# One batch of ring addresses per loop round, in place of an address instruction before each operation, in a streaming RMSNorm + swish kernel

## The chip, the cores and the metric

The kernel runs on one core of one Trainium2 chip. The metric is the device time of one execution in microseconds. Three runs of the kernel before gave 159.98, 160.04 and 160.12 us; their median, 160.04 us, is the time that the change is measured against. One further execution was recorded by the hardware profiler, and all rows of the profile come from it: it took 159.97 us, of which the span from the first to the last instruction is 158.5 us.

## What is computed

The input x has 16 x 1024 rows of 512 float32. Each row is divided by its root mean square, multiplied by gamma (512 values), and passed through swish:

```python
rms = np.sqrt(np.mean(x ** 2, axis=-1, keepdims=True) + eps)
x_norm = x / rms * gamma
return x_norm * (1.0 / (1.0 + np.exp(-x_norm)))
```

Input and output are 33.55 MB each, so 67.1 MB have to cross between the chip's memory and the core.

## The kernel before, in words

The 16,384 rows are laid over the 128 partitions, 128 rows to a partition. A row of a partition is 512 floats (2 KB). On the chip stands one buffer, `xb`, a ring with room for 96 of the 128 rows of every partition; rows 96 to 127 go into the places of rows 0 to 31 once these have been stored. All work on a row is done in place in `xb`.

The transfers are all issued by SyncE (SP), in an order written out by hand (lines 30 to 41): seven loads fill the ring (rows 0-3, 4-7, 8-15, 16-31, 32-63, 64-91, 92-95), the first two of them ahead of the program's opening barrier. SP then waits until the load of rows 64-91 has landed (line 156), issues the stores of rows 0-15 and 16-31 (line 138), waits for each of these two before it issues the loads that reuse its places (line 132), waits for the load of rows 112-123 (line 156), and then issues the five last stores: rows 32-63, 64-95, 96-111, 112-119 and 120-127. Every store also waits on the semaphore `s_swish`, which counts finished units; a unit is 4 rows of every partition. The five last stores need 16, 24, 28, 30 and 32 of the 32 units. At the end SP waits for the stores to land (line 277).

The compute is software pipelined over the 32 units. For each unit:

- `square` on ScalarE (ACT), lines 191 to 201: rows 2 and 3 are each squared and summed by an activation of 512 elements whose output goes to a scratch tile `junk` (line 193); rows 0 and 1 are squared by one activation of 1024 elements into the PSUM tile `sq` (line 199). It waits on `s_land`, which TensorE's queue raises as loads land (line 166).
- `sums` on VectorE (DVE), line 220: sums `sq` over the two rows into `ms`.
- `power` on GpSimd (POOL), lines 175 and 182: `rstd` = (ms + eps) to the power -1/2.
- `norm` on DVE, line 230: four operations, one for each row, multiply the row by its `rstd` and by gamma in place.
- `swish` on ACT, line 205: one activation of 2048 elements in place, which raises `s_swish`.

ACT and DVE each run a hardware loop of 10 rounds with `turn` = 3 units to the round (lines 244 and 256); two units are squared ahead of the loop and two are finished behind it (`lead` = 2). In a round ACT does, three times over, the square of unit m + 2 and then the swish of unit m; DVE does the sums of unit m + 1 and then the norm of unit m. At the end of a round each engine takes the round's counts off its semaphores (line 161), adds one to its counter and branches back.

Since the ring place of a unit depends on the round, the operations in the loops address `xb` through a register. `now` and `then` are row numbers held in registers; `rows(at, n)` makes a slice out of one, and the compiler puts ahead of each operation a fused register instruction that multiplies the row number out to a byte address (it shows as FUSED_REGOPS in the trace, with the line number of the operation that it serves). The units ahead of and behind the loops have fixed addresses and no such instructions.

Of the kernel before, what the change touches and what calls it, by code (L numbers as in the profile page):

```python
# [9 lines left out]
def kernel(  # L10
# [7 lines left out]
    nc = tc.nc  # L18
    P = nc.NUM_PARTITIONS
    AF = mybir.ActivationFunctionType  # L20
    ALU = mybir.AluOpType
    fp32 = mybir.dt.float32
# [3 lines left out]
    R, D = xf.shape  # L26

    groups = [16, 16, 32, 32, 16, 16]
    ring = 96
# [13 lines left out]
    cn = 4  # L43
    n_sq = 2
    turn = 3
    lead = 2
# [14 lines left out]
    per_ring = ring // (turn * cn)  # L61
# [15 lines left out]
    def sbuf(name, shape, dt=fp32):  # L77
        return nc.alloc_sbuf_tensor(name, shape, dt).ap()

    xb = sbuf("xb", [P, ring, D])  # L80
    gamma4 = sbuf("gamma4", [P, D])
    gamma_sb = sbuf("gamma_sb", [P, D])
    neg_half = sbuf("neg_half", [P, cn])
# [2 lines left out]
    rstd = sbuf("rstd", [P, turn, cn])  # L86
    sq = [nc.alloc_psum_tensor(f"sq{i}", [P, n_sq, D], fp32).ap() for i in range(turn)]
    junk = [nc.alloc_psum_tensor(f"junk{i}", [P, D], fp32).ap() for i in range(2)]
    junk += [sbuf(f"junk{i}", [P, D]) for i in range(2, turn * (cn - n_sq))]

    ld = [nc.alloc_semaphore(f"ld{t}") for t in range(len(loads))]
# [5 lines left out]
    s_land = nc.alloc_semaphore("s_land")  # L97
# [8 lines left out]
    def need(ins, sem, value):  # L106
        return ins.wait_op(sem, value, "sem-ge")
# [36 lines left out]
    for t in range(early):  # L144
# [3 lines left out]
        at = next(  # L148
            i for i, other in enumerate(entry)
            if other.engine == mybir.EngineType.SP  # L150
            and isinstance(other, mybir.InstDrain)
        )
# [7 lines left out]
    def take(queue, sem, n):  # L160
        need(queue.nop(nofuse=True), sem, n).then_inc(sem, -n)
# [24 lines left out]
        ).then_inc(s_rstd, 1)  # L186

    def rows(at, n):
        return xb[:, at : at + n, :] if isinstance(at, int) else xb[:, bass.ds(at, n), :]

    def square(k, at, sem, count, accs):
        for j in range(n_sq, cn):
            acc = nc.scalar.activation(  # L193
                out=junk[(k % turn) * (cn - n_sq) + j - n_sq], in_=rows(at + j, 1)[:, 0, :], func=AF.Square,
                scale=inv_d**0.5, accum_out=ms[:, k % turn, j : j + 1],
            )
            if j == n_sq:
                need(acc, sem, count)
        nc.scalar.activation(  # L199
            out=sq[k % turn], in_=rows(at, n_sq), func=AF.Square, scale=inv_d**0.5,  # L200
        ).then_inc(s_sq, 1)

    def swish(at, nth):
        need(
            nc.scalar.activation(out=rows(at, cn), in_=rows(at, cn), func=AF.Silu),  # L205
            s_norm, nth + 1,
        ).then_inc(s_swish, 1)
# [5 lines left out]
    nc.scalar.preload_act_table_set("silu_and_others")  # L213
    for k in range(lead):
        assert landings[k] == [k]
        square(k, k * cn, ld[k], 16, k * (cn - n_sq))

    def sums(k, nth):
        need(
            nc.vector.tensor_reduce(  # L220
                out=ms[:, k % turn, 0:n_sq], in_=sq[k % turn], op=ALU.add,
                axis=mybir.AxisListType.X,
            ),
            s_sq, nth + 1,
        ).then_inc(s_sum, 1)

    def norm(k, at, nth):
        for j in range(cn):
            row = rows(at + j, 1)[:, 0, :]
            ins = nc.vector.scalar_tensor_tensor(  # L230
                out=row, in0=row, scalar=rstd[:, k % turn, j : j + 1], in1=gamma_sb,
                op0=ALU.mult, op1=ALU.mult,
            )
            if j == 0:
                need(ins, s_rstd, nth + 1)
        ins.then_inc(s_norm, 1)
# [4 lines left out]
    ).then_inc(s_gamma, 1)  # L241
    nc.vector.wait_ge(s_gamma, 1)

    with nc.Fori(0, rounds, engines=[mybir.EngineType.Activation]) as i:  # L244
        now = nc.scalar.snap((i % per_ring) * (turn * cn))
        then = nc.scalar.snap(((i + 1) % per_ring) * (turn * cn))
        for m in range(turn):
            behind = now + (m + lead) * cn if m + lead < turn else then + (m + lead - turn) * cn
            square(m + lead, behind, s_land, m + 1, lead * (cn - n_sq) + m * (cn - n_sq))
            swish(now + m * cn, m)  # L250
        take(nc.scalar, s_land, turn)
        take(nc.scalar, s_norm, turn)
    for m in range(lead):
        swish((rounds * turn + m) * cn % ring, m)

    with nc.Fori(0, rounds, engines=[mybir.EngineType.DVE]) as i:
        now = nc.vector.snap((i % per_ring) * (turn * cn))
        for m in range(turn):
            sums(m + 1, m + 1)
            norm(m, now + m * cn, m)  # L260
        take(nc.vector, s_sq, turn)
        take(nc.vector, s_rstd, turn)
    sums(K - 1, 1)
    for m in range(lead):
        norm(rounds * turn + m, (rounds * turn + m) * cn % ring, m)
# [47 lines left out]
```

## Time and profile before

| | |
|---|---|
| median of three runs | 160.04 us (159.98 to 160.12) |
| the profiled execution | 159.97 us |
| its span, first to last instruction | 158.5 us |
| ACT busy | 129.7 us (82% of the span) |
| DVE busy | 124.5 us (79%) |
| POOL busy | 65.4 us (41%) |
| moved by DMA | 67.12 MB, mean 424 GB/s over the span |
| end of the last swish | 143.8 us into the span |

Busy times are those of the engines' own operations. Register, branch, semaphore and DMA-issuing instructions are handled by an engine's sequencer and are not counted as busy; where a view lists them, the engine's name carries a q (ACTq, DVEq, SPq). "DMA" in the views by windows is the busy share of the core's 16 DMA engines, where 1.00 is all of them all the time; a packet counts in the window in which it is booked, so that short windows read over or under the mean.

### The profile page before, as it was taken

The page shows a single profiled execution, that of the slowest core. Times are in us where ns is not written, and L with a number is a line of the kernel's source. Part 1 is how long each engine was busy: PE and PEld are TensorE (multiplying, and loading weights), DVE is VectorE, ACT ScalarE, POOL GpSimd, SP SyncE. Part 2 cuts the span into 40 slices and gives each one's busy share as a digit, 9 for nine tenths or more (in the row PEclk, how much of TensorE's full clock was granted, in tenths as well). Part 3 has the DMA queues.
Part 4 walks back from the last instruction along what each step waited for, and adds up shares of the span by engine and source line. Part 5 has one row for each costly group of instructions (what it writes and reads, how often), then busy time and mean ns, then how long its engine had stood idle before and what let it go on. Part 6 is the DMA issues. An engine that isn't in the chain of part 4 may idle for free. (4 is left out here: it accounts for less than half of the span.)

```text
span 158.5 us, 896 instructions
## 1 busy us (share of the span) xinstructions
DVE 124.5 (79%) x162; ACT 129.7 (82%) x193; POOL 65.4 (41%) x70
## 2 busy tenths in 40 slices
DVE  0187968999199999999999999999999999980000
ACT  0949959995599999999999999999999999663000
POOL 1053555555055555555555555555555555500000
DMA  7999997989999969999999999896996996999996
GB/s 256 445 492 397 397 612 314 529 380 414 463 463 463 405 279 440 513 414 397 397 455 463 407 428 529 364 529 281 513 529 265 529 513 281 405 496 414 389 414 265
DMA packets 2456, 67.12 MB, mean 424 GB/s; under 512 B 276, under 2 KB 276, under 8 KB 280
## 3 DMA queue, kind: packets, MB, share of 16 engines
q1 hardware_dynamic: 2448, 67.11, 98.6%
q10 hardware_dynamic: 8, 0.01, 0.0%
HBM read 33.56 MB, written 33.55 MB: 424 GB/s over the span
## 5 line engine op out<-in xcount | busy, mean ns | idle before, releaser
L230 DVE SCALAR_TENSOR_TENSOR xb<-xb,rstd,gamma_sb 128x512 f32 (+1 forms) x128 | 87.3, 744 | 0.0
L205 ACT ACTIVATE xb<-xb (+1 forms) x32 | 60.9, 1903 | 2.8 <-DVE xb L230 2.8
L220 DVE TENSOR_REDUCE ms<-sq 128x2 f32<-128x1024 f32 x32 | 39.2, 1224 | 17.4 <-ACT sq L199 14.2
L175 POOL TENSOR_SCALAR aeps<-ms 128x4 f32<-128x4 f32 x32 | 20.6, 643 | 69.0 <-DVE ms L220 69.0
L182 POOL TENSOR_TENSOR rstd<-aeps,neg_half 128x4 f32<-128x4 f32 x32 | 44.1, 1378 | 2.7
L193 ACT ACTIVATE junk<-xb 128x512 f32 (+1 forms) x64 | 38.6, 603 | 7.7 <-PEq L166 7.5
L199 ACT ACTIVATE sq<-xb 128x1024 f32 (+1 forms) x32 | 32.2, 1005 | 0.0
L193 ACT ACTIVATION_READ_ACCUMULATOR junk<-xb 128x1 f32 x64 | 11.9, 186 | 0.0
L213 ACT ACT_TABLE_LOAD x1 | 1.3, 1283 | 3.6 <-issue 3.6
L168 POOL MEMSET gamma<- 128x512 f32 x1 | 0.5, 524 | 1.5 <-POOLq L75 1.5
L240 DVE STREAM_SHUFFLE gamma_sb<-gamma 128x512 f32<-128x512 f32 x1 | 0.7, 719 | 0.0
L294 POOL MEMSET const-float32-0.0<- 128x1 f32 x1 | 0.1, 98 | 0.2 <-issue 0.2
L294 POOL MEMSET const-uint8-127<- 128x1 uint8 x1 | 0.1, 102 | 0.0
L294 POOL MEMSET const-bfloat16-1.0<- 128x1 bf16 x1 | 0.1, 101 | 0.0
L169 POOL MEMSET neg_half<- 128x4 f32 x1 | 0.1, 101 | 0.0
L294 POOL MEMSET const-float32-1.0<- 128x1 f32 x1 | 0.1, 98 | 0.0
L240 DVE LOAD_MASK_SELECT gamma_sb<-gamma x1 | 0.0, 14 | 0.0
## 6 DMA issues: line engine op xcount, KB each, us to landing
out_dram<-xb SPq DMA_DIRECT2D x3, 4096.0 KB, 19.5
xb<-in_x_dram SPq DMA_DIRECT2D x2, 4096.0 KB, 19.6
xb<-in_x_dram SPq DMA_DIRECT2D x1, 7168.0 KB, 54.8
xb<-in_x_dram SPq DMA_DIRECT2D x4, 1024.0 KB, 13.0
out_dram<-xb SPq DMA_DIRECT2D x2, 2048.0 KB, 15.5
xb<-in_x_dram SPq DMA_DIRECT2D x1, 3072.0 KB, 16.9
xb<-in_x_dram SPq DMA_DIRECT2D x1, 2048.0 KB, 10.2
out_dram<-xb SPq DMA_DIRECT2D x2, 23.9
```

The costliest lines, as they stand in the source:

```text
L168: nc.gpsimd.memset(gamma4, 0.0).then_inc(s_zero, 1)
L169: nc.gpsimd.memset(neg_half, -0.5).then_inc(s_half, 1)
L175: nc.gpsimd.tensor_scalar(out=aeps[:, m, :], in0=ms[:, m, :], scalar1=eps_f, scalar2=None, op0=ALU.add,),
L182: nc.gpsimd.tensor_tensor(out=rstd[:, m, :], in0=aeps[:, m, :], in1=neg_half, op=ALU.pow),
L193: acc = nc.scalar.activation(out=junk[(k % turn) * (cn - n_sq) + j - n_sq], in_=rows(at + j, 1)[:, 0, :], func=AF.Square, scale=inv_d**0.5 ...
L199: nc.scalar.activation(out=sq[k % turn], in_=rows(at, n_sq), func=AF.Square, scale=inv_d**0.5,).then_inc(s_sq, 1)
L205: nc.scalar.activation(out=rows(at, cn), in_=rows(at, cn), func=AF.Silu),
L213: nc.scalar.preload_act_table_set("silu_and_others")
L220: nc.vector.tensor_reduce(out=ms[:, k % turn, 0:n_sq], in_=sq[k % turn], op=ALU.add, axis=mybir.AxisListType.X,),
L230: ins = nc.vector.scalar_tensor_tensor(out=row, in0=row, scalar=rstd[:, k % turn, j : j + 1], in1=gamma_sb, op0=ALU.mult, op1=ALU.mult,)
L240: nc.vector.stream_shuffle(gamma_sb, gamma4, [0] * 32), s_gld, 16
L294: nc = _bacc.Bacc("TRN2", target_bir_lowering=False, num_devices=1)
```

## The change

The ring is allocated as bytes and viewed as float32, so that an operation can be given a byte address that already stands in a register. `now` and `then` become byte offsets. At the head of each round a new function, `addresses`, asks for all the addresses of the round at once, and the compiler packs up to six of the additions into one fused register instruction. The operations then use the finished registers.

```diff
+    row = D * mybir.dt.size(fp32)
+    xb8 = sbuf("xb", [P, ring * row], mybir.dt.uint8)
+    xb = xb8.bitcast(fp32).rearrange("p (r d) -> p r d", d=D)
...
     def rows(at, n):
-        return xb[:, at : at + n, :] if isinstance(at, int) else xb[:, bass.ds(at, n), :]
...
+        if isinstance(at, int):
+            return xb[:, at : at + n, :]
+        base, c = at
+        return bass.AP(
+            xb8.tensor, base + c * row, xb8[:, 0 : n * row].ap
+        ).bitcast(fp32)
+
+    def addresses(queue, base, offsets):
+        for c in offsets:
+            nc.lower_val(base + c * row + 16512, [queue])
...
+    span = turn * cn
     with nc.Fori(0, rounds, engines=[mybir.EngineType.Activation]) as i:
-        now = nc.scalar.snap((i % per_ring) * (turn * cn))
-        then = nc.scalar.snap(((i + 1) % per_ring) * (turn * cn))
+        now = nc.scalar.snap((i % per_ring) * (span * row))
+        then = nc.scalar.snap(((i + 1) % per_ring) * (span * row))
+        ahead = [
+            (now, m * cn) if m < turn else (then, m * cn - span)
+            for m in range(lead, lead + turn)
+        ]
+        addresses(mybir.EngineType.Activation, now, [m * cn for m in range(turn)])
+        for base, c in ahead:
+            addresses(
+                mybir.EngineType.Activation, base,
+                [c + j for j in [0, *range(n_sq, cn)]],
+            )
         for m in range(turn):
-            behind = now + (m + lead) * cn if m + lead < turn else then + (m + lead - turn) * cn
-            square(m + lead, behind, s_land, m + 1, lead * (cn - n_sq) + m * (cn - n_sq))
-            swish(now + m * cn, m)
+            square(m + lead, ahead[m], s_land, m + 1)
+            swish((now, m * cn), m)
...
     with nc.Fori(0, rounds, engines=[mybir.EngineType.DVE]) as i:
-        now = nc.vector.snap((i % per_ring) * (turn * cn))
+        now = nc.vector.snap((i % per_ring) * (span * row))
+        addresses(mybir.EngineType.DVE, now, range(span))
         for m in range(turn):
             sums(m + 1, m + 1)
-            norm(m, now + m * cn, m)
+            norm(m, (now, m * cn), m)
```

In the built program a round on ACT has 3 fused register instructions, all at its head, in place of 11 fused ones and 2 single ones that stood between its operations. A round on DVE has 3, at its head and so ahead of its first sum, in place of 12, one ahead of each multiply. On DVE a move that copied the loop counter at the head of the round is gone. The instructions of SP, POOL and TensorE are the same in both programs, the 17 transfers and their waits among them, and so are the operations of ACT and DVE, their order, their waits and the place of every tile.

More of the change, by code (lines that the diff above doesn't have):

```diff
@@ L78, in sbuf @@
         return nc.alloc_sbuf_tensor(name, shape, dt).ap()
-    xb = sbuf("xb", [P, ring, D])
+    row = D * mybir.dt.size(fp32)
+    xb8 = sbuf("xb", [P, ring * row], mybir.dt.uint8)
+    xb = xb8.bitcast(fp32).rearrange("p (r d) -> p r d", d=D)
     gamma4 = sbuf("gamma4", [P, D])
@@ L188, in rows, with down, square @@
     def rows(at, n):
-        return xb[:, at : at + n, :] if isinstance(at, int) else xb[:, bass.ds(at, n), :]
-    def square(k, at, sem, count, accs):
+        if isinstance(at, int):
[4 more added lines that the diff above has]
+        ).bitcast(fp32)
+    def down(at, j):
+        return at + j if isinstance(at, int) else (at[0], at[1] + j)
+    def addresses(queue, base, offsets):
+        for c in offsets:
+            nc.lower_val(base + c * row + 16512, [queue])
+    def square(k, at, sem, count):
         for j in range(n_sq, cn):
             acc = nc.scalar.activation(
-                out=junk[(k % turn) * (cn - n_sq) + j - n_sq], in_=rows(at + j, 1)[:, 0, :], func=AF.Square,
+                out=junk[(k % turn) * (cn - n_sq) + j - n_sq], in_=rows(down(at, j), 1), func=AF.Square,
                 scale=inv_d**0.5, accum_out=ms[:, k % turn, j : j + 1],
@@ L215 @@
         assert landings[k] == [k]
-        square(k, k * cn, ld[k], 16, k * (cn - n_sq))
+        square(k, k * cn, ld[k], 16)
     def sums(k, nth):
@@ L228, in norm @@
         for j in range(cn):
-            row = rows(at + j, 1)[:, 0, :]
+            one = rows(down(at, j), 1)
             ins = nc.vector.scalar_tensor_tensor(
-                out=row, in0=row, scalar=rstd[:, k % turn, j : j + 1], in1=gamma_sb,
+                out=one, in0=one, scalar=rstd[:, k % turn, j : j + 1], in1=gamma_sb,
                 op0=ALU.mult, op1=ALU.mult,
```

## The prediction

> **What bounds the kernel now.** I read the page first, then the DMA share by windows, then the waits of SP, then the issue and landing of each late store.
>
> ```profile
> span 158.5 us, 896 instructions
> ...
> DVE 124.5 (79%) x162; ACT 129.7 (82%) x193; POOL 65.4 (41%) x70
> ...
> DMA packets 2456, 67.12 MB, mean 424 GB/s; under 512 B 276, under 2 KB 276, under 8 KB 280
> ...
> L230 DVE SCALAR_TENSOR_TENSOR xb<-xb,rstd,gamma_sb 128x512 f32 (+1 forms) x128 | 87.3, 744 | 0.0
> ```
>
> ```profile
> core 0: us, DVE busy (x) ACT busy (x) POOL busy (x), PEclk, DMA share, GB/s
> 2.00:156.00 154.00, 124.52 (x162) 129.68 (x193) 65.15 (x66) 1.00 1.00 432
> ```
>
> No engine is busy all the time, but the 16 DMA engines are: their share is 1.00 over 154 of the 158.5 us, at 432 GB/s. So the transfers set the time as long as they don't run out of issued work. Which of them could? Those that wait for compute: the stores. I read the five late ones singly.
>
> ```profile
> SPq L138 <- ACT xb L205: 45.1, 4, 15.6
> ...
> SPq L277 <- DMA out_dram<-xb: 14.2, 3, 4.8
> ```
>
> ```profile
> 97.32 0.34 SPq L138 DMA_DIRECT2D out_dram<-xb  x1
> 113.28 0.34 SPq L138 DMA_DIRECT2D out_dram<-xb  x1
> 129.25 0.33 SPq L138 DMA_DIRECT2D out_dram<-xb  x1
> 137.23 0.33 SPq L138 DMA_DIRECT2D out_dram<-xb  x1
> 143.85 0.33 SPq L138 DMA_DIRECT2D out_dram<-xb  x1
> ```
>
> ```profile
> out_dram<-xb SPq DMA_DIRECT2D x1, 22.0
> out_dram<-xb SPq DMA_DIRECT2D x1, 25.7
> out_dram<-xb SPq DMA_DIRECT2D x1, 4096.0 KB, 19.5
> out_dram<-xb SPq DMA_DIRECT2D x1, 2048.0 KB, 16.3
> out_dram<-xb SPq DMA_DIRECT2D x1, 2048.0 KB, 14.6
> ```
>
> These are the five last stores, in order: when each is issued, and its us from issue to landing. SP waits 45.1 us for swish, which looks like compute holding the stores up. It isn't: the store issued at 97.32 lands at 97.32 + 22.0 = 119.3, and the next was issued at 113.28, 6.0 us earlier. The others are issued 9.7 (113.28 + 25.7 - 129.25), 11.5 and 9.7 us before the one ahead of them lands. After the last swish SP still waits 14.2 us for stores alone. Each late store queues behind another.
>
> How late may one be? A transfer needs some time from issue to its first bytes:
>
> ```profile
> xb<-in_x_dram SPq DMA_DIRECT2D x1, 1024.0 KB, 4.8
> ```
>
> This is the first load, on idle engines: 1.05 MB at 432 GB/s are 2.4 of its 4.8 us, so the start and finish cost at most 2.4. The tightest spare time is then 6.0 - 2.4 = 3.6 us, at the store of rows 64-95, which needs 24 swishes. Compute can lose 3.6 us up to there for nothing, and whatever it gains buys nothing.
>
> **The change, part by part.** Address instructions removed and added:
>
> ```profile
> L230 DVEq FUSED_REGOPS  x120: 69/69/125, 9.7 to 131.8; - x120
> L244 ACTq FUSED_REGOPS  x10: 102/103/136, 7.5 to 123.7; - x10
> L193 ACTq FUSED_REGOPS  x50: 55/55/121, 12.2 to 131.4; - x50
> L199 ACTq FUSED_REGOPS  x30: 52/55/55, 12.4 to 131.6; - x30
> L205 ACTq FUSED_REGOPS  x20: 52/54/55, 12.5 to 127.8; - x20
> ```
>
> Over the 10 rounds these are 12 a round on DVE and 11 on ACT (two single register instructions besides). Removed is 12 x 69 ns = 0.83 us of DVE's sequencer a round and 103 + 10 x 55 ns = 0.65 us of ACT's. What is this worth to the engines? The chain of waits, across the end of a round on ACT:
>
> ```profile
> 111.73 0.10 ACTq L244
> 111.83 0.03 issue
> ...
> 112.03 0.09 issue
> ...
> 112.24 0.05 ACTq L205
> 112.29 0.87 issue
> 113.16 1.32 ACT junk L193 x4
> ```
>
> ```profile
> 111.34 1.91 ACT L205 ACTIVATE xb<-xb  x1
> ```
>
> The second fence is the swish ahead of it. The register instructions at the head of the round run from 111.73 to 112.29, while that swish, started at 111.34, still has to 113.25 to go; 0.87 us after them the next square starts on its heels (an operation starts a little before the one ahead has ended). So on ACT the removal is worth 0. On DVE the loop can be held against the two units behind it, whose addresses are fixed:
>
> ```profile
> 107.44 1.23 DVE L220 TENSOR_REDUCE ms<-sq 128x2 f32<-128x1024 f32 x1
> 108.58 2.73 DVE L230 SCALAR_TENSOR_TENSOR xb<-xb,rstd,gamma_sb 128x512 f32 x4
> 111.41 1.22 DVE L220 TENSOR_REDUCE ms<-sq 128x2 f32<-128x1024 f32 x1
> ...
> 135.36 1.23 DVE L220 TENSOR_REDUCE ms<-sq 128x2 f32<-128x1024 f32 x1
> 136.50 5.38 DVE L230 SCALAR_TENSOR_TENSOR xb<-xb,rstd,gamma_sb 128x512 f32<-128x512 f32 x8
> ```
>
> From the start of the sum to the first multiply are 1.14 us with register addresses (107.44 to 108.58) and 1.14 without (135.36 to 136.50). One multiply follows another at (2.73 - 0.74) / 3 = 0.66 us with them and at (5.38 - 0.74) / 7 = 0.66 us without, 0.74 being the time of one. So on DVE, too, the removal is worth 0.
>
> The batch moved to the head is the cost side. On ACT it is 3 instructions of up to six steps; the dearest seen is 136 ns, and the chain shows 0.03 to 0.09 us between two of them, so at most 3 x 0.23 = 0.7 us, against 0.56 now. Begun at 111.73 it ends by 112.4, 0.7 us ahead of the square at 113.16: cost 0, covered by the swish. Without that cover it would be 0.7 us a round.
>
> On DVE the batch newly stands ahead of the round's first sum, and the sum, the four multiplies, and through `s_sum` POOL's power are queued behind it.
>
> ```profile
> L256 DVEq MOVE  x1: 36/36/36, 108.5 to 108.5; - x1
> ```
>
> The loop's head is reached at 108.5, because the sequencer runs ahead of the engine: the first multiply of the unit before starts only at 108.58. Three instructions at the dearest seen, 125 ns, with 0.07 us between them (four start between 107.5 and 107.9), take 0.6 us; DVE's never had more than five steps, so I allow twice that, 1.2. The sum behind them starts at 111.41, 2.9 us after the head. Cost 0, covered by the multiplies; without the cover 0.6 us a round (bound 1.2). In the first round no multiplies run ahead of the batch, but a slip there, at most the 1.2 us, ends in a wait for a load that ACT has anyway:
>
> ```profile
> 41.29 0.63 ACT L193 ACTIVATE junk<-xb 128x512 f32 x1 [3.28 <-PEq L166]
> ```
>
> This is the last wait of its kind; it is 3.28 us long, and takes up what was lost before it.
>
> The sum: 158.5 + 0 + 0, and with the 159.97 - 158.5 = 1.5 us outside the span 159.97. The runs' median is 0.07 above that execution, so I say 160.0. What this measurement tells from no change is about 0.2%, 0.32 us.
>
> [...]
>
> **The rivals.**
>
> *Slower: the batches are exposed on both engines.* If the engines can't start the first operation until the batch behind the branch is through and the branch is reached later than I read, each round is longer by up to 0.7 (ACT) + 0.6 (DVE), since the swish, the square, the sum and the multiplies wait on one another in a ring. From 41.29 to 113.28 stand 72 us, 6 rounds of 12 us (three units of 3.97, 107.44 to 111.41): 6 x 1.3 = 7.8 us, less 3.6 spare, gives 164.2. It decides from 3.6 / 6 = 0.6 us a round; one engine alone, 0.6 or 0.7, gives 160.0 to 160.6. Against it: both heads lie under running work by 0.7 and by 2.3 us. [...]
>
> *Faster: a shorter program starts or ends sooner.* Of 26 register instructions in the two loops' bodies 6 are left. The time outside the span is 1.5 us, and if a third of it went with the program's length the time would be 159.5. For it: nothing in the span forbids it. Against it: SP's instructions are the same, and the first load is SP's first instruction.
>
> *The change is made and compute gets faster.* The stores would be issued sooner and wait longer: 160.0, the forecast's time.
>
> **How the numbers follow.** No change 0.82 (that compute moves either way inside its spare time is in it), exposed batches 0.10, an earlier start or end 0.06, and 0.02, half to either side, for transfers that run at another rate under another timing of the engines. So slower 0.11, faster 0.07, same 0.82. The no-change case spans 159.7 to 160.4; I stretch it to 159.6 and, for one engine's batch exposed, to 160.5.
>
> **What would show it.** Right: a DMA share of 1.00 from 2 to 156 us, the last store landing near 158.5, register instructions of ACT and DVE falling from 23 fused ones a round to 6, the sum's start still 1.14 us ahead of the first multiply and units still 3.97 to 4.0 us apart. Wrong: a DMA share that falls between 113 and 120 us (the slower rival), a store of rows 64-95 issued after 116.9 (113.28 + 3.6), or a span unchanged with another time outside it (the faster one).

## The result, and the profile after

| | before | after |
|---|---|---|
| time, median (lowest to highest), 19 runs each | 160.07 us (159.89 to 160.23) | 159.61 us (159.47 to 159.91) |
| ratio, 95% interval | | 0.9974 [0.9967, 0.998] |
| the profiled execution: its time, its span | 159.97, 158.5 us | 159.47, 158.2 us |
| recorded instructions | 896 | 696 |

The changed kernel is faster by 0.46 us, 0.2 to 0.33% by the interval. That is a little more than the 0.2% that I called no change, so the forecast "no change" fell, by a small margin, although 159.61 still lies inside the range I had stated. The views shown of before look like this now. First the page, then busy time by windows (DVE, ACT, POOL, clock, DMA share, GB/s), then the waits of SP (us in total, times, longest):

```profile
span 158.2 us, 696 instructions
...
DVE 124.5 (79%) x162; ACT 129.7 (82%) x193; POOL 65.4 (41%) x70
...
DMA packets 2456, 67.12 MB, mean 424 GB/s; under 512 B 276, under 2 KB 276, under 8 KB 280
```

```profile
core 0: us, DVE busy (x) ACT busy (x) POOL busy (x), PEclk, DMA share, GB/s
2.00:156.00 154.00, 124.53 (x162) 129.67 (x193) 65.17 (x66) 1.00 1.00 433
```

```profile
SPq L140 <- ACT xb L219: 45.2, 4, 15.7
...
SPq L302 <- DMA out_dram<-xb: 13.8, 3, 4.8
```

The engines do the same operations in the same busy time, the DMA engines have a share of 1.00 in both, and SP still waits 45 us for swish. Only the last figure moved: SP's final waits for the stores fell from 14.2 to 13.8 us. So I read the five late stores again: the timeline of their issue on SP, then us from issue to landing.

```profile
97.19 0.34 SPq L140 DMA_DIRECT2D out_dram<-xb  x1
113.28 0.34 SPq L140 DMA_DIRECT2D out_dram<-xb  x1
129.25 0.33 SPq L140 DMA_DIRECT2D out_dram<-xb  x1
137.23 0.33 SPq L140 DMA_DIRECT2D out_dram<-xb  x1
143.85 0.33 SPq L140 DMA_DIRECT2D out_dram<-xb  x1
```

```profile
out_dram<-xb SPq DMA_DIRECT2D x1, 21.9
out_dram<-xb SPq DMA_DIRECT2D x1, 25.4
out_dram<-xb SPq DMA_DIRECT2D x1, 4096.0 KB, 19.2
out_dram<-xb SPq DMA_DIRECT2D x1, 2048.0 KB, 16.0
out_dram<-xb SPq DMA_DIRECT2D x1, 2048.0 KB, 14.3
```

Four of the five are issued at the same hundredth of a microsecond as before. Compute sets the time of issue, so compute isn't faster. But each transfer lands 0.1 to 0.3 us sooner after its issue (22.0, 25.7, 19.5, 16.3, 14.6 before). That is one part of the gain. The other stands outside the span: 159.97 - 158.5 = 1.5 us before, 159.47 - 158.2 = 1.3 us after.

Are the address instructions hidden, as I argued? DVE around a round's end, and the register instructions at the head of ACT's and DVE's rounds (ns min/median/max, first and last start):

```profile
107.44 1.22 DVE L234 TENSOR_REDUCE ms<-sq 128x2 f32<-128x1024 f32 x1
108.58 2.73 DVE L244 SCALAR_TENSOR_TENSOR xb<-xb,rstd,gamma_sb 128x512 f32 x4
111.42 1.23 DVE L234 TENSOR_REDUCE ms<-sq 128x2 f32<-128x1024 f32 x1
```

```profile
L259 ACTq FUSED_REGOPS  x10: 102/103/133, 7.4 to 123.7; - x10
L203 ACTq FUSED_REGOPS  x20: 70/90/109, 7.6 to 124.0; - x20
L280 DVEq FUSED_REGOPS  x10: 128/134/135, 9.2 to 119.9; - x10
L203 DVEq FUSED_REGOPS  x20: 65/79/99, 9.4 to 120.2; - x20
...
L280 DVEq FUSED_REGOPS  x1: 134/134/134, 107.9 to 107.9; - x1
L203 DVEq FUSED_REGOPS  x2: 65/79/93, 108.1 to 108.2; - x2
```

The three rows of DVE stand where they stood, with 1.14 us from the sum to the first multiply. Six fused instructions a round are left of 23. DVE's batch of this round lies at 107.9 to 108.3, 3.1 us ahead of the sum at 111.42 that is queued behind it. ACT's in the chain of waits:

```profile
111.73 0.10 ACTq L259
111.83 0.03 issue
111.86 0.10 ACTq L203
111.97 0.03 issue
111.99 0.07 ACTq L203
112.06 1.10 issue
113.16 1.32 ACT junk L207 x4
```

It ends at 112.06 instead of 112.29, and the square behind it starts at 113.16 as before, on the heels of the swish. The gain therefore comes neither from ACT nor from DVE. What ties it to this change? I had two candidates, the rate of the transfers and the time outside the span.

### The profile page after: what moved, and what is told of

The parts are those of the page before. It is cut to its first block, busy times and chain, and to the rows that moved or that the text cites. A ratio compares the mean times of both kernels' runs of the same rounds, so it can differ in the third digit from the quotient of the medians.

```text
span 158.2 us, 696 instructions
## 1 busy us (share of the span) xinstructions
DVE 124.5 (79%) x162; ACT 129.7 (82%) x193; POOL 65.4 (41%) x70
## 5 line engine op out<-in xcount | busy, mean ns | idle before, releaser
L234 DVE TENSOR_REDUCE ms<-sq 128x2 f32<-128x1024 f32 x32 | 39.2, 1225 | 17.4 <-ACT sq L213 14.2
## 6 DMA issues: line engine op xcount, KB each, us to landing
xb<-in_x_dram SPq DMA_DIRECT2D x2, 4096.0 KB, 19.5
out_dram<-xb SPq DMA_DIRECT2D x2, 2048.0 KB, 15.1
```

What stands on the lines that cost most here:

```text
L234: nc.vector.tensor_reduce(out=ms[:, k % turn, 0:n_sq], in_=sq[k % turn], op=ALU.add, axis=mybir.AxisListType.X,),
```

## The experiments

All edits are to the changed kernel. Times are medians, and each ratio is against the kernel before on the same chip. The expectations call the explanations by letters: A, each executed instruction costs one DMA ring time (a ring is here the row of packets that one of the 16 DMA engines works off without a gap); B, the address instructions of ACT and DVE themselves cost time; C, the number of instructions counts wherever they run; D, the cheaper form of an address is the gain; E, the length of the program counts; F, straight code that has to be fetched made the first added instructions slow.

**Is it the number of instructions, or their place?** Without the calls of `addresses`, each operation computes its own address again, right ahead of itself:

```diff
-        addresses(mybir.EngineType.Activation, now, [m * cn for m in range(turn)])
-        for base, c in ahead:
-            addresses(
...
-        addresses(mybir.EngineType.DVE, now, range(span))
```

> The changed kernel without the batches: each operation again has its own address instruction ahead of it, now a single addition to a byte offset. Theory A: 24 register instructions a round against 6, nearly as many records as before, so 160.0 us. Theory D (the gain comes from the cheaper form of the address, not from the number): 159.6 us. Theory B with the batch as its cause: 160.0 us too, but then with units more than 4.0 us apart.

159.95 us (159.8 to 160.21, 12 runs), ratio 0.9998 [0.9988, 1.0007]: the gain is gone. The register instructions of DVE's multiplies and its timeline:

```profile
L244 DVEq ALU_OP  x110: 40/40/52, 10.0 to 132.0; - x110
L244 DVEq FUSED_REGOPS  x10: 87/88/95, 9.7 to 123.7; - x10
```

```profile
107.67 1.23 DVE L234 TENSOR_REDUCE ms<-sq 128x2 f32<-128x1024 f32 x1
108.81 2.73 DVE L244 SCALAR_TENSOR_TENSOR xb<-xb,rstd,gamma_sb 128x512 f32 x4
111.64 1.23 DVE L234 TENSOR_REDUCE ms<-sq 128x2 f32<-128x1024 f32 x1
```

An instruction here is cheaper than one of before (40 ns against 69), there are about as many (876 recorded against 896), and units are 3.97 us apart as ever. So the cheaper form isn't the gain. But of the 0.34 us lost against 159.61 only some 0.1 lies in the span; 0.24 lies outside it (1.55 against 1.31 us, in a table below), so this run alone doesn't show what an instruction costs under the stores.

**Do hidden instructions cost anything, and where?** TensorE does nothing in this kernel but pass on the landing of loads. Given 200 waits that are already met, it executes them beside everything else. In one kernel they follow the landing of load 9 and ran from 100.6 to 122.2 us, under the late stores; in the other they follow load 3 (`i == 3`), from 22 us on.

```diff
             need(nc.tensor.nop(nofuse=True), ld[i], 16).then_inc(s_land, units)
+        if i == 9:
+            for _ in range(200):
+                need(nc.tensor.nop(nofuse=True), ld[i], 16)
```

> The changed kernel with 200 waits that are already met, on TensorE's queue (idle otherwise), right after the last load lands at about 99 us, while stores are in flight. Theory A (each executed instruction costs one of the 16 DMA rings about 2.4 ns while stores run; the gain came from 186 fewer instructions between 10 and 143 us): 200 x 2.4 ns = 0.48 us, so 160.1 us, with ACT's and DVE's rows unchanged and the last landing later by about 0.5 us than the first ring's allows. Theory B (the address instructions of ACT and DVE themselves cost time there): no change, 159.6 us.

> The same 200 waits, but after the fourth load has landed (about 22 us), while only loads run. Theory A as the rings' landings suggest (hardly any lag before 60 us): 159.6 to 159.7 us. Theory C (the number of instructions in the whole program counts, wherever they run, for instance at its end): 160.0 to 160.1 us. Theory B: 159.6 us.

160.66 us (160.05 to 161.24, 12 runs), ratio 1.0034 [1.0017, 1.0051], and 160.68 (160.56 to 161.03, 6 runs), ratio 1.0046 [1.0028, 1.0064]. Both lose some 1.06 us against 159.61, so place doesn't tell them apart. But written out, the 200 instructions come with a fetch, of which the pages of the changed kernel and the one before show none: the trace of the late one has a 16 KB packet marked as instructions at 126.2 us, which takes 0.94 us, and the data packets ahead of it and behind it are longer by 590 and 398 ns. The early one has such a packet at 46.7 us, of 1.06 us, and 498 ns on the one behind it. That is 1.9 and 1.6 us on one ring, more than either kernel lost. The pair measures two costs at once and decides nothing; the next kernels put the waits into a loop of 20 trips, and of 40 in a second kernel; both run under the late stores.

```diff
+        if i == 9:
+            with nc.Fori(0, 20, engines=[mybir.EngineType.PE]):
+                for _ in range(10):
+                    need(nc.tensor.nop(nofuse=True), ld[i], 16)
```

> The changed kernel with the 200 met waits on TensorE's queue as a loop of 20 x 10 from about 99 us, so that the program is hardly longer (12 instructions) while some 240 more are executed. Theory A (executed instructions): 240 x 2.4 ns = 0.58 us, 160.2 us, one ring's packets longer by about 25 ns each per ten records. Theory F (the length of the straight code, which has to be fetched in blocks through the same rings, made the first two experiments slow): 159.6 us. Both: between 160.2 here and the 160.66 of the written-out waits, the difference being the fetch.

> The late loop with 40 x 10 waits, some 480 instructions more between 99 and about 150 us. Theory A is linear: 480 x 2.4 ns = 1.15 us, 160.8 us. Theory F: 159.6 us, as the loop of 20.

160.11 us (160.02 to 160.64, 12 runs), ratio 1.001 [1.0, 1.0019], and 160.64 (160.55 to 160.79, 4 runs), ratio 1.0042 [1.0026, 1.0058]. Over 159.61 that is 0.50 us for 241 more recorded instructions, and 1.03 for 481: 2.1 ns each, and linear (2.4 and 2.3 ns by the ratios, which compare on one chip). The kernel of 400 in the windows, and its late stores' us from issue to landing:

```profile
core 0: us, DVE busy (x) ACT busy (x) POOL busy (x), PEclk, DMA share, GB/s
2.00:156.00 154.00, 124.55 (x162) 129.68 (x193) 65.14 (x66) 1.00 1.00 431
```

```profile
out_dram<-xb SPq DMA_DIRECT2D x1, 26.1
out_dram<-xb SPq DMA_DIRECT2D x1, 4096.0 KB, 20.1
out_dram<-xb SPq DMA_DIRECT2D x1, 2048.0 KB, 17.0
out_dram<-xb SPq DMA_DIRECT2D x1, 2048.0 KB, 15.4
```

Four of them, issued at 113.30 to 143.88 us (113.28 to 143.85 in the changed kernel), land 0.7, 0.9, 1.0 and 1.1 us later. It is the same place as the gain, with the other sign. No engine is busier and the DMA share is still 1.00: the transfers themselves last longer.

The early loop (20 trips, `i == 3`) was to show the same number of instructions under loads.

> The same loop, but from 22 us, under the loads. Theory A with a cost only under stores: 159.6 to 159.7 us, and no lag of a ring at the landing of rows 32-63 (41 us). Theory A with a cost at any time: 160.1 to 160.2 us. Theory F: 159.6 us.

164.82 us (164.63 to 165.02, 5 runs), ratio 1.0299 [1.0285, 1.0313]. The loop didn't finish before the next landing at 41 us but ran until 51.2, and TensorE passed that landing on late. So it tests something else, the spare time of compute. The square that waits for it, the store that it decides, and the windows around that store:

```profile
51.38 0.63 ACT L211 ACTIVATE junk<-xb 128x512 f32 x1 [13.12 <-PEq L168]
```

```profile
123.37 0.34 SPq L140 DMA_DIRECT2D out_dram<-xb  x1
```

```profile
core 0: us, DVE busy (x) ACT busy (x) POOL busy (x), PEclk, DMA share, GB/s
...
113.00:118.00 5.00, 4.76 (x7) 5.00 (x8) 2.04 (x2) 1.00 0.97 419
118.00:124.00 6.00, 5.89 (x9) 6.00 (x10) 3.14 (x4) 1.00 0.00 0
124.00:156.00 32.00, 27.25 (x37) 27.11 (x36) 13.22 (x13) 1.00 1.01 434
```

Compute is 10.1 us late (41.29 before), the store of rows 64-95 10.1 us late (113.28), and no packet starts from 118 to 124: on most rings the last one ends by 118.7 us, and the first of the late store starts at 124.21, 0.84 us after its issue. The time is 5.2 us longer, so 10.1 - 5.2 = 4.9 us of the delay were free; by the spans of the two profiled executions (163.7 and 158.2 us) it is 4.6.

With half the trips the loop ends before the landing at 41 us:

```diff
+        if i == 3:
+            with nc.Fori(0, 10, engines=[mybir.EngineType.PE]):
...
```

> The changed kernel with a loop of 10 x 10 met waits on TensorE's queue from 22 us, which ends before the load of rows 32-63 lands at 41 us and so delays nothing. Theory A with a cost at any time: 120 x 2.1 ns = 0.25 us, 159.85 us. Theory A with a cost under stores alone: 159.6 us, and no lag of a ring at 41 us.

159.52 us (159.32 to 160.36, 12 runs), ratio 0.9975 [0.9958, 0.9993]: no cost of 121 more instructions under loads is to be seen. Under stores they would be 0.25 us at 2.1 ns each, which the interval could just hide; the packets are clearer. From 22 to 36 us this kernel executes 179 instructions and the changed one 63, and in both no ring's packets are longer than usual by more than 19 ns in sum.

**Would fewer still be faster?** Two kernels: the loops written out with fixed addresses (495 recorded instructions), and two rounds to a loop's body, 5 trips (616).

```diff
-    with nc.Fori(0, rounds, engines=[mybir.EngineType.Activation]) as i:
...
+    for k in range(K - lead):
+        square(k + lead, (k + lead) * cn % ring, s_land, k + 1)
+        swish(k * cn % ring, k)
```

```diff
-    span = turn * cn
+    many = 2 * turn
+    span = many * cn
+    trips = rounds // 2
```

> The changed kernel with the three loops written out: fixed addresses, no register instructions, no branches and no taking of counts off the semaphores. Theory A: some 18 instructions a round fewer over the 3.6 rounds under the late stores, about 65 x 2.4 ns = 0.16 us, so 159.4 to 159.5 us. Theory B: 159.6 us or, if what is left of the batches costs time, up to 0.2 us less through earlier ends of units. Theory E (a shorter program is what counts): slower than 159.6 us, since the written-out program is longer.

> The changed kernel with two rounds (6 units) to a loop body and 5 trips: one set of taking counts, counter, branch and batch of addresses for 6 units, so about 80 executed instructions fewer than the changed kernel, and a program longer by about 60 but without a block of code fetched under way as in the written-out kernel. Theory A: 159.61 - 80 x 2.4 ns = 159.4 us. Theory F: 159.6 us or a little more. Theory B (the batches at the head cost time): up to 0.2 us less, with shorter units.

160.15 us (159.93 to 160.33, 12 runs), ratio 1.0007 [0.9997, 1.0017], and 160.14 (159.81 to 160.86, 12 runs), ratio 1.0008 [0.9995, 1.0022]. Neither keeps the gain, and theory A, which had both faster than 159.61, missed. The trace of the first shows packets of 8 KB marked as instructions at 33.2, 49.0, 82.7 and 126.2 us, and data packets beside them longer by 341, 660, 220 and 141 ns; that of the second has one at 40.4 us, with 361 ns. The pages of both list these packets under a queue of their own, q14, beside q1 with the data, and still the ring that carries them pays: data stop there while the fetched packet runs (309 to 325 ns), and the next data packet is longer. How much of the two times it explains isn't settled, because the stretch from 77 to 83 us, where stores give way to loads, varies too (0.20 to 0.55 us over the four profiles of before and after), and with two rounds to a body 0.23 of the 0.53 us lost lies outside the span.

The last kernel cuts instructions without more code: one multiply over the four rows of a unit in place of four. It takes the factor of the first row for all four and multiplies by the data instead of gamma, so it computes something else.

```diff
-        for j in range(cn):
-            one = rows(down(at, j), 1)
...
+        four = rows(at, cn)
+                out=four, in0=four, scalar=rstd[:, k % turn, 0:1], in1=four,
```

> The changed kernel with one DVE operation over the four rows of a unit in place of four, and one batch of 3 addresses for DVE in place of 12 in three instructions. It multiplies all four rows by the first row's factor and by themselves, not by gamma, so its output is another. DVE's busy time stays about the same; 116 executed instructions fewer and the program shorter. Theory A: 159.61 - 116 x 2.1 ns = 159.35 us. Theory F: 159.6 us or a little less. Theory B: 159.6 us.

159.64 us (159.31 to 160.77, 12 runs), ratio 0.9978 [0.9958, 0.9998].

```profile
L244 DVE SCALAR_TENSOR_TENSOR xb<-xb,rstd (+1 forms) x32 | 75.0, 2343 | 1.2 <-POOL rstd L184 1.2
```

DVE's multiplies fell from 87 to 75 us, which again buys nothing. Of the 116 instructions saved only 34 lie under the late stores (172 to 138). At 2.1 to 2.7 ns these are worth under 0.1 us, too little for this measurement to see.

**Is it the chip?** Both kernels were run again beside the last two:

> The kernel before, unchanged, once more, for a second profile on the same chip as the next three. All theories: 160.0 us. Theory A: again one ring that falls behind the others between 99 and 143 us by some 0.6 us, packet after packet.

> The changed kernel, unchanged, once more. All theories: 159.6 us, 0.4 us under the kernel before on this chip as well; if it is within 0.2 us of it here, the difference belongs to the chip or the day and not to the change. Theory A: the ring behind the others loses about 0.45 us between 99 and 143 us.

160.05 us (159.77 to 160.5, 12 runs), ratio 1.0 [0.9985, 1.0014], and 159.6 (159.51 to 160.59, 12 runs), ratio 0.9978 [0.9958, 0.9999]. The difference repeats. Late stores of the changed kernel, us from issue to landing:

```profile
out_dram<-xb SPq DMA_DIRECT2D x1, 25.6
out_dram<-xb SPq DMA_DIRECT2D x1, 4096.0 KB, 19.3
out_dram<-xb SPq DMA_DIRECT2D x1, 2048.0 KB, 16.2
out_dram<-xb SPq DMA_DIRECT2D x1, 2048.0 KB, 14.4
```

In the kernel before, on the same chip, they took 26.3, 20.0, 16.9 and 15.1.

**What happens inside the transfers.** The 64 KB packets of the late stores take 2418 ns each. In the first profiles of both kernels all packets on 15 of the 16 rings keep to that; on one, every packet is 14 to 69 ns longer. In other executions the other rings have some extra as well, up to 0.24 us where nothing is fetched, but one still stands out. A packet doesn't name its ring: the rings are put together from packets that follow one another without a gap (with 200 waits late in a loop two rings come into step at 119 us, and the sum follows the longer packets). The extra time of that ring between 101.5 and 137.5 us, summed from its packets, beside the instructions executed in that stretch:

```
kernel                       instructions   extra on the ring   ns each
before, before again           228, 228        601, 488 ns      2.6, 2.1
after, after again             172, 171        464, 456         2.7, 2.7
each op its own address        222             478              2.2
loops written out              119             304              2.6
one multiply a unit            138             380              2.8
100 waits early                172             355              2.1
200 waits early, written out   174             474              2.7
two rounds to a body           155             399              2.6
200 waits late, written out    363             931              2.6
200 waits late, in a loop      403             944              2.3
400 waits late, in a loop      469            1217              2.6
200 waits early, in a loop     179             155              0.9
```

From 119 to 469 instructions the extra goes from 304 to 1217 ns. The last row is an exception that I can't explain: in that execution no ring stands out under the late stores (the next has 128 ns), although under its first stores, from 60.6 to 77 us, one has 214 ns for 83 instructions (228 for 110 in the kernel before).

The 16 rings share each late store (rows 64-95: 128 packets of 64 KB, 8 to a ring), and it lands when the last ring is done: the final store at 143.85 + 14.6 = 158.45 us before and 143.85 + 14.3 = 158.15 after, the last ring at 158.43 and 158.11. In the first profiles of both kernels this ring is the last: in the kernel before it is done 0.70 us behind the one before it (157.73, 158.43 us), in the changed kernel 0.52 (157.59, 158.11). Under the loads at 41 and 60 us the gap is 0.02 to 0.05. It is the last in the two late loops, too. It isn't always the last: in the second profiles of both kernels, and in those of an address to each operation, one multiply a unit and 100 waits early, another ring ended 0.08 to 0.55 us behind it. That ring had little or no extra, but had begun its late stores 0.8 to 1.1 us after the median ring. In each of these kernels the profiled execution took longer than the median.

**And outside the span.** The time less the span, over every timed run that has a span:

```
kernel                       runs   mean span   time less span: mean (lowest to highest)
before, three chips           87      158.5     1.49 to 1.51  (1.41 to 1.57)
after                         19      158.3     1.31  (1.27 to 1.36)
after again                   12      158.4     1.31  (1.27 to 1.36)
each op its own address       12      158.4     1.55  (1.50 to 1.60)
two rounds to a body          12      158.6     1.54  (1.31 to 1.67)
loops written out             12      158.8     1.31  (1.27 to 1.36)
200, 400 waits in a loop    12, 4  158.8, 159.4 1.32, 1.30  (1.27 to 1.35)
```

A span is on record to 0.1 us, which alone spreads single differences by 0.05 either way. Apart from the kernel with two rounds to a body, which has 1.31 once and 1.44 to 1.67 otherwise, no run lies between 1.36 and 1.41. The 0.18 us between before and after is a step, not noise. It doesn't follow the number of executed instructions (400 more change nothing) nor the length of the program (the written-out one has 1.31). In both profiles of before 0.15 us of it lies between two of the program's last semaphore events, 185 ns apart instead of 34. The kernel with an address to each operation has the 34 and loses its time elsewhere outside the span. Why is open.

## Why the prediction was right or wrong

- *What bounds the kernel*: right. The DMA share is 1.00 in both, and 12 us less of DVE's multiplies bought nothing.
- *The removed address instructions are worth 0 on ACT and on DVE*: right. The units, the 1.14 us and the times of issue stayed.
- *The batches are covered*: right. ACT's ends 1.10 us ahead of its square and DVE's 3.1 us ahead of its sum.
- *3.6 us of spare time*: right in kind, short in size. The early loop measured 4.6 to 4.9. From 6.0 less these, 1.1 to 1.4 us, follows that I took too much for a transfer's start and finish with my bound of 2.4; 0.84 us of it is the start, read from the packets.
- *Slower by exposed batches*: it didn't happen, but its path is real. The early loop made compute late by more than its spare time, and the DMA engines ran dry ahead of the store that I had named.
- *The sum, "158.5 + 0 + 0, and with the 159.97 - 158.5 = 1.5 us outside the span 159.97"*: this step failed, in two terms. That 159.61 lies inside the range of 159.6 to 160.5 is luck: it does so by 0.01 us, and I had stretched the lower end from 159.7 to 159.6 without a mechanism.

The first is that an instruction hidden on its engine costs nothing. Under the late stores one ring was longer by 2.1 to 2.8 ns for each executed one, in all profiles but one: linear in the two late loops, and not to be seen under loads. The change takes 56 instructions out of the stretch that I summed, worth 0.12 to 0.16 us; in the first two profiles the gap of the last ring fell by 0.70 - 0.52 = 0.18. I read the mean share of 16 engines, which is 1.00 either way, and not which of them ends last.

The second is the constant outside the span, which fell by 0.18 us. That is the place of my faster rival, which I gave 0.06 because SP's instructions are the same. Its mechanism, a shorter program, isn't what the written-out loops and the 400 waits show. The sign that I had set for it, "a span unchanged with another time outside it", came in half: the span changed as well.

The account of the 0.46 us: 0.18 outside the span, some 0.15 on the ring, and some 0.1 besides. Where this last part can lie is to be seen in the first two profiles, whose spans differ by 0.32 us. From 99 us on the ring that ends last has 0.18 us less extra (0.56 against 0.74), and it begins its late stores 0.14 us earlier (99.02 against 99.16), 0.05 of which all rings share. That the change causes this earlier start isn't shown. The stretch from 77 to 83 us alone cost 0.25 and 0.51 us in the two profiles of before, 0.20 and 0.55 in those of after, so single executions differ by more than that.

One limit holds for all of it: every execution with a span was taken with its instructions recorded. What the extra on the ring is spent on, and whether it remains without the recording, no run shows.

## What to carry to other kernels

Where the DMA engines are saturated as here (a share of 1.00 from 2 to 156 us), "hidden on its engine" isn't yet "free" (0.50 us for 241 instructions on TensorE): look at when each ring of a store ends, not at the mean share. Prices are small (2 to 3 ns for an instruction under stores, in recorded executions), so it matters only for what is left in a kernel that transfers bound. Longer code gave the gain back here, written out and with twice the loop's body alike (160.15 and 160.14 us against 159.61). And compare time less span between two kernels before taking it for a constant (here 1.49 to 1.51 us against 1.31).

## What was unexpected of the hardware

- In 13 of 14 profiles one ring of 16 was slower under the late stores by 2.1 to 2.8 ns for each instruction executed, TensorE's met waits included; under loads (22 to 36 us) none was.
- The time outside the span differs by kernel: 1.30 to 1.33 us in some, 1.49 to 1.55 in others.
- Fetched code shows in the transfers: beside packets of 8 or 16 KB marked as instructions data packets lasted 141 to 660 ns longer.
- Where stores give way to loads (77 to 83 us), packets of 32 KB, whose median is 1213 ns, took up to 1.64 and 1.69 us in the first profiles of before and after, and this cost 0.20 to 0.55 us of a ring's time, by the mean of all 16, over the four profiles of the two kernels.
